# An encoder trunk on one core: operands spread, rows transposed later, factors at the additions, products three key blocks behind scores

## The chip, the core and the metric

The kernel runs on one core of a Trainium2 chip. The core has TensorE (PE), which multiplies matrices into PSUM; VectorE (DVE), ScalarE (ACT) and GpSimd (POOL), which work on rows of 128 partitions; and SyncE (SP), which mostly issues DMAs. Each engine works through its own queue in order, and semaphores let one engine wait for another. The metric is the time of one execution in microseconds (us), as the device tells it.

## What is computed

One layer, 2048 positions of 1024 channels, all in float32. The part of the reference that matters:

```python
xn = rms_norm(x, mix_norm_g[l])
q, k, v, f_logit, z = jnp.split(xn @ w_in[l], [...], axis=-1)
log_f = jax.nn.log_sigmoid(f_logit + b_f[l])
attn = forgetting_attention(q, k, v, log_f)      # 8 heads of 64, causal, logit + c[t] - c[s]
sgu = spatial_gating(jax.nn.gelu(z, approximate=False),
                     sgu_ln_g[l], sgu_ln_b[l], w_s[l], b_s[l])
merged = jnp.concatenate([rms_norm(attn, out_norm_g[l, :D_ATTN]),
                          rms_norm(sgu, out_norm_g[l, D_ATTN:])], axis=-1)
x = x + merged @ w_out[l]
xn = rms_norm(x, ffn_norm_g[l])
gate, up = jnp.split(xn @ w_gate_up[l], 2, axis=-1)
x = x + (jax.nn.silu(gate) * up) @ w_down[l]
return rms_norm(x, final_norm_g)
```

`c` is the running sum of `log_f`. The two `rms_norm`s inside `merged` each give one factor per position: one for the attention half, one for the gating half.

## The kernel before

**Exactness.** A matmul takes operands of a shorter mantissa, so every operand is split into a high part (a cast, L128, on ACT) and a low part (the operand minus the high part, L131, on DVE), and a product is three matmuls: high by high, high by low, low by high.

**Stages.** First q, k, v are projected (to about 310 us of the span). Then follow attention and the gating branch, interleaved (310 to 870 us). The output projection runs from about 870 to 1100 us, overlapping the end of attention. The rest is the feed-forward part, built from seven products per two-by-two block instead of eight (L1742), whose operands are sums and differences of blocks.

**Attention (L727 to L795, loop at L1260).** The loop goes over 320 steps `(head, query chunk of 512, key block of 128)`. In step n, `qk` makes a score tile [128 keys, 512 queries] with two matmuls (L735, L736) into one of two PSUM banks `mx_ps`, which the maxima of later heads (`one_max`, L360) share. ACT takes Exp into `Pt` (L738) and casts it to `Ph` (L128); DVE subtracts to `Pl` (L131); on a diagonal block POOL masks `Ph` and then `Pl` (L748). `pv_of` multiplies by values (L768, L770, L773) into the bank `tp`. It is called `DEPTH` steps after `qk`. `NPH`, `NPL` and `NPT` are the numbers of `Ph`, `Pl` and `Pt` tiles. Keys and values lie in five sets of buffers; `plan_loads` frees a set `DEPTH + 1` steps after its last score, and `keys_until` issues the loads of the next at most `LEAD` = 14 steps ahead of their use. `fin` (L777) closes a head and, after the last head of a chunk, turns the sums into reciprocals (L793) and stores them to `RD` (L794).

**Gating branch.** `gates` (L1008) runs beside attention, paced by n, and fills PE: `z_proj` projects four chunks q, first for the half that is normalised and mixed (`v_side`, stored to `GD`), then for the half that multiplies it (`u_side`, L977). `at_u` (L889) hooks loads to the place `(q, cc, k)` in that projection, among them the load of `GD[q]` into `zvh` (L904), which `u_side` needs at L985. `u_side` multiplies by the mixed half, takes squares, makes the factor `rs`, scales the rows by it (L995), transposes them (L998) and stores them to `ST`.

**Output projection.** `out_prep` loads the transposed rows of one tile of 128 positions (`ST`, `AT`) and the reciprocals, makes the attention half's factor `o["r"]` (squares L1097, sums L1099 and L1100, product L1105) and splits the rows. Tiles 0 and 1 are prepared inside the attention loop from n = `OPEN` = 260 on. `out_tiles` (L1192) runs the products (L1190) in slots of three matmuls, 16 slots a tile; `out_add` (L1179) adds the gating half plainly (L1182) and the attention half times `o["r"]` (L1184). After a tile `out_done` (L1152) stores the row, takes its squares (L1156), its factor (L176), scales it (L1162) and, `NY - 1` calls later, transposes it (L1169) and stores it to `XT` for the feed-forward part. These calls (`posts`) come on every second slot.

**First feed-forward operands.** `first_operands` (L1666) loads the four blocks of the first positions from `XT`, makes the operands R4, R1, R3 in 16 parts spread over the slots, and then R0, R2 and at last R5, R6. The main loop at L1700 calls it on every `FE`-th slot, from tile `FT` = 9 on; what is left is forced when the first half of the last two tiles is done.

**Order.** The framework lays out each engine's queue when the program is built, from the order in which the code issues instructions and from what is ready by its own reckoning. `behind(i, ...)` (L110) keeps what is issued inside it behind i on i's engine.

## Time and profile before

| | us |
|---|---|
| median of 3 runs | 2358.18 (2357.91 to 2358.35) |
| the profiled execution | 2357.63 |
| its span, first to last instruction | 2355.9 |
| PE busy in the span | 2329.2 (99%) |
| DVE busy | 1689.4 (72%) |
| ACT busy | 1059.9 (45%) |
| POOL busy | 607.9 (26%) |
| granted PE clock, mean | 0.998 |

Rows of a group name the line, the engine, the operation, out<-in and its shape, then xcount, busy us, the mean ns of one, and the idle time of the engine just before them with what ended most of it. Rows of the timeline begin with the start and the length in us and end, in brackets, with the idle time before and its releaser. Rows of waits have the total in us, the number of times and the longest. A busy PE is drawn longer than it is, since matmuls are pipelined and their ends modelled. Idle time of an engine that isn't the bound costs nothing by itself.

### The profile page before, as it was taken

What the parts mean: (1) busy time and instruction counts of PE and PEld (TensorE: products, weight loads), DVE (VectorE), ACT (ScalarE), POOL (GpSimd) and SP (SyncE); (2) the same over time, 40 slices, a digit from 0 to 9 for tenths busy, and PEclk for the clock granted to TensorE, in tenths of its full rate; (3) what the DMA queues carried; (4) which work ended last, traced back from release to release, by engine and by line L of the source; (5) the groups of instructions that cost most, each with busy time, mean ns of one, the idle gap of its engine ahead of it and who ended that gap; (6) DMA issues with size and microseconds to landing.
All of it is one profiled execution on the core that took longest, in us unless ns stands there. A gap on an engine that the chain in (4) does not pass through costs nothing.

```text
span 2355.9 us, 31718 instructions
## 1 busy us (share of the span) xinstructions
PE 2329.2 (99%) x10566; PEld 1891.3 (80%) x10566; DVE 1689.4 (72%) x2799; ACT 1059.9 (45%) x1774; POOL 607.9 (26%) x704
## 2 busy tenths in 40 slices
PE   9999999999999999999999999999999999999998
PEld 7778777777777778878888888888888878888886
DVE  6658668888888677567665766866666586685788
ACT  5322138767788776344323233533323252332433
POOL 1100012122211232222322323232323234343431
PEclk9999999999999999999999999999999999999999
DMA  8845667656687775773445544725444355574554
GB/s 271 297 154 189 211 201 208 184 146 169 177 215 239 219 230 178 229 221 126 114 137 162 151 149 129 234 77 145 126 143 143 90 191 193 190 254 170 194 193 150
DMA packets 375947, 423.89 MB, mean 180 GB/s; under 512 B 23956, under 2 KB 277588, under 8 KB 371816
## 3 DMA queue, kind: packets, MB, share of 16 engines
q1 hardware_dynamic: 359800, 378.62, 52.6%
q0 software_dynamic: 7616, 27.33, 3.3%
q10 hardware_dynamic: 8368, 15.91, 1.9%
q8 instruction: 85, 1.39, 0.3%
q14 instruction: 78, 0.64, 0.1%
HBM read 280.87 MB, written 140.91 MB: 179 GB/s over the span
## 4 chain that ended last, share of the span: by engine, by line
PE 89%; DVE 4%; ACT 2%; DMA 2%; issue 2%; POOL 1%; POOLq 0%; ACTq 0%; SPq 0%; DVEq 0%
PE pp L1742 51%; PE mm L575 7%; PE z L927 6%; PE pp L1190 4%; PE mm L457 4%; PE mx_ps L360 2%; PE tp L768 2%; PE tp L773 2%; PE mx_ps L735 2%; PE mx_ps L736 2%; PE oz L1190 2%; PE tp L770 1%; DVE wl L131 1%; DVE Pl L131 1%; PE z L968 0%
## 5 line engine op out<-in xcount | busy, mean ns | idle before, releaser
L128 ACT CAST wh<-raw 128x512 fp32r<-128x512 f32 (+2 forms) x492 | 304.1, 621 | 726.9 <-PE pp L1742 612.9
L131 DVE TENSOR_TENSOR wl<-raw,wh 128x512 fp32r<-128x512 f32 (+2 forms) x496 | 375.7, 765 | 27.5 <-ACT wh L128 27.0
L1742 PE MATMUL pp<-wl,wh 128*128 128x512 f32 x1056 | 325.3, 389 | 1.1 <-ACT u L1490 1.0
L1742 PE MATMUL pp<-wh,wh 128*128 128x512 f32 x1056 | 325.2, 389 | 0.0
L1433 POOL TENSOR_TENSOR raw<-raw 128x512 f32<-128x512 f32 (+1 forms) x124 | 169.2, 1366 | 551.9 <-DMA raw<-in_w_gu_dram 302.5
L131 DVE TENSOR_TENSOR Pl<-Pt,Ph 128x512 fp32r<-128x512 f32 (+1 forms) x320 | 194.9, 614 | 71.6 <-ACT Ph L128 70.4
L1742 PEld LDWEIGHTS pp<-wl,wh 128*128 128x128 f32 x1056 | 198.1, 188 | 42.9 <-ACT u L1490 1.4
L1742 PEld LDWEIGHTS pp<-wh,wh 128*128 128x128 f32 x1056 | 198.2, 188 | 41.0
L738 ACT ACTIVATE Pt<-mx_ps 128x512 f32<-128x512 f32 (+1 forms) x320 | 168.8, 532 | 118.4 <-PE mx_ps L736 112.8
L1742 PE MATMUL pp<-wl,wl 128*128 128x512 f32 x528 | 205.4, 389 | 0.0
L1742 PE MATMUL pp<-wh,wl 128*128 128x512 f32 x528 | 205.4, 389 | 0.0
L1433 DVE TENSOR_TENSOR raw<-raw,raw 128x512 f32<-128x512 f32 (+1 forms) x112 | 136.6, 1221 | 84.1 <-POOL raw L1433 81.0
L927 PE MATMUL z<-wh,xz 128*128 128x512 f32 x496 | 188.7, 397 | 0.0
L128 ACT CAST Ph<-Pt 128x512 fp32r<-128x512 f32 (+1 forms) x320 | 175.5, 556 | 19.7 <-PE tp L770 4.8
L362 DVE TENSOR_REDUCE mx<-mx_ps 128x1 f32<-128x512 f32 x192 | 130.1, 683 | 20.6 <-PE mx_ps L360 19.7
L748 POOL TENSOR_SCALAR_AFFINE_SELECT Ph<-Ph 128x128 fp32r<-128x128 f32 x128 | 51.0, 398 | 300.9 <-DVE Pl L131 252.0
L768 PE MATMUL tp<-Ph,V 128*128 128x512 f32 (+1 forms) x320 | 118.7, 371 | 4.8 <-POOL Ph L748 2.5
L360 PE MATMUL mx_ps<-D,A 66*128 66x512 f32 (+2 forms) x320 | 118.7, 373 | 1.2 <-DVE mx L365 0.8
L773 PE MATMUL tp<-Pl,V 128*128 128x512 f32 (+1 forms) x320 | 118.4, 370 | 1.1 <-POOL Pl L748 1.0
L735 PE MATMUL mx_ps<-A,D 74*128 74x512 f32 (+1 forms) x320 | 118.0, 369 | 1.1 <-ACT Pt L738 1.1
L736 PE MATMUL mx_ps<-B,C 128*128 128x512 f32 (+1 forms) x320 | 117.4, 367 | 0.0
L1742 PEld LDWEIGHTS pp<-wl,wl 128*128 128x128 f32 x528 | 99.1, 188 | 20.6
(355 smaller groups left out, 5287.8 us busy)
## 6 DMA issues: line engine op xcount, KB each, us to landing
raw<-in_w_gu_dram SPq DMA_DIRECT2D x88, 512.0 KB
xz<-XS SPq DMA_DIRECT2D x31, 1024.0 KB
HD<-hT SPq DMA_DIRECT2D x44, 512.0 KB
SM<-xa SPq DMA_DIRECT2D x30, 512.0 KB
D<-KH SPq DMA_DIRECT2D x112, 128.0 KB
XA<-xa SPq DMA_DIRECT2D x27, 512.0 KB
sg<-SM SPq DMA_DIRECT2D x12, 1024.0 KB
raw<-HD SPq DMA_DIRECT2D x24, 512.0 KB
```

Source lines behind the costliest of these rows:

```text
L128: return nc.scalar.copy(o, i) if eng is nc.scalar else eng.tensor_copy(o, i)
L131: return eng.tensor_tensor(o, i, f(h), ALU.subtract)
L360: last_mx.append(nc.tensor.matmul(pm[:, 0:n], lhs, Dt[0 : lhs.shape[0], 0:n], start=True, stop=True))
L575: mm = nc.tensor.matmul(pm, a, b, start=n == 0, stop=n == 3 * KT - 1)
L735: nc.tensor.matmul(st[:, off:], Dt[:, b * P : (b + 1) * P], A[:, off:], start=True, stop=False)
L736: nc.tensor.matmul(st[:, off:], C[:, b * P : (b + 1) * P], B[:, off:], start=False, stop=True)
L738: nc.scalar.activation(Pt[:, off:], st[:, off:], AF.Exp)
L768: nc.tensor.matmul(pv[:, off:], V[:, 0:P], Ph[:, off:], start=kb == 0, stop=False)
L773: nc.tensor.matmul(pv[:, off:], V[:, 0:P], Pl[:, off:], start=False, stop=kb == 4 * j + 3)
L927: nc.tensor.matmul(pz, xz[a][:, k, :], w[b][:, k, :], start=n == 0, stop=n == 3 * KT - 1)
L1433: return (nc.vector if e == "v" else nc.gpsimd).tensor_tensor(o, a, b, op)
L1742: nc.tensor.matmul(pm, a[:, k, :], b[:, k, :], start=on is None and k == 0 and e == 0, stop=k == it.kh - 1 and e == 2, skip_group_check=n ...
```

## The change

It has these parts:

1. `DEPTH` 2 to 3, `NPH` and `NPL` 3 to 4, `NPT` 4 to 3: a product comes three steps behind its score, with four tiles of high and low weights and three of `Pt`. `nd` and `lv` in `fin` share one tile of 128 partitions.
2. `rsg` keeps the gating half's factors of all positions. `u_side` no longer scales rows; `out_add` applies `rsg` to the gating half's product as it applies `o["r"]` to the other's.
3. `NY` 4 to 5, and `posts` also move on at every slot while more than one is waiting: rows are transposed one call later.
4. The first operands start when the first eight tiles' transposed rows are stored, instead of at tile 9, and take a part on every fifth slot. The last sums and R5, R6 are put behind the last row's squares (on ACT) and scaling (on DVE).
5. Tiles 0 and 1 wait six calls instead of four for their loads, and four instead of six between squares and factor. `fin` gives one call between the reciprocal and its store. The loads of `GD[q]` move within the projection.

```diff
-DEPTH = 2
+DEPTH = 3
-NPH = 3
-NPL = 3
+NPH = 4
+NPL = 4
-NPT = 4
+NPT = 3
-NY = 4
+NY = 5
-FT = 9
-FE = 4
+FE = 5
...
+    rsg = T(cst, [P, NB], F32, "rsg")
...
     def fin(h, j):
-        nd, lv = T(p2, [DH, CH], F32, "nd", bufs=1), T(p2, [DH, CH], F32, "lv", bufs=1)
+        both = T(p2, [P, CH], F32, "nd", bufs=1)
+        lv, nd = both[0:DH], both[DH:P]
...
             nc.vector.reciprocal(sr, sr)
+            yield
             ld(RD[j].rearrange("h (a t) -> (h a) t", t=H * CH // P), sr)
...
-        if at[1:] == ((2, 0) if at[0] else (3, 4)):
+        if at[1:] == ((3, 4), (2, 0), (2, 0), (3, 0))[at[0]]:
             m = mixes[at[0]] = T(p2z, [P, 4, CH], F32, "zvh", bufs=1)
             ld(m, GD[at[0]])
...
-        rs = rsqrt(p2, ss, 1.0 / 512, "rs", n=4)
-        yield
+        rsqrt(p2, ss, 1.0 / 512, "rs", n=4, r=rsg[:, 4 * q : 4 * q + 4])
...
         for cc in range(4):
-            nc.vector.tensor_scalar_mul(zr[:, cc, :], zr[:, cc, :], rs[:, cc : cc + 1])
...
-        for _ in range(4):
+        for _ in range(4 if space is None else 6):
             yield
...
             yield from squares()
-            for _ in range(6):
+            for _ in range(4):
                 yield
             yield from factor(p2)
...
-        nc.scalar.activation(xn, xt, AF.Square, accum_out=ss)
+        E["sq"] = nc.scalar.activation(xn, xt, AF.Square, accum_out=ss)
...
-        nc.vector.scalar_tensor_tensor(xn, xt, r, E["ffb"], ALU.mult, ALU.mult)
+        E["xn"] = nc.vector.scalar_tensor_tensor(xn, xt, r, E["ffb"], ALU.mult, ALU.mult)
...
             ld(XT[t // 8][2 * g + q][:, :, sl], xo)
+            E["xt"] = t + g
             yield
...
     def out_add(xs, ps, t, k):
-        if k > 3:
-            nc.vector.tensor_tensor(xs, xs, ps, ALU.add)
-        else:
-            nc.vector.scalar_tensor_tensor(xs, ps, o[t]["r"], xs, ALU.mult, ALU.add)
+        r = rsg[:, t : t + 1] if k > 3 else o[t]["r"]
+        nc.vector.scalar_tensor_tensor(xs, ps, r, xs, ALU.mult, ALU.add)
...
-                        if k % 2 == 0 and posts and next(posts[0], 0) == 0:
+                        if (k % 2 == 0 or len(posts) > 1) and posts and next(posts[0], 0) == 0:
                             posts.pop(0)
...
         yield "wait"
-        tt("v", b11, b11, b12, ALU.add)
-        tt("v", b21, b21, b11, ALU.subtract)
-        R[5] = keep_as(5, b21)
-        R[6] = keep_as(6, b22)
+        with behind(E["sq"], E["xn"]):
+            tt("v", b11, b11, b12, ALU.add)
+            tt("v", b21, b21, b11, ALU.subtract)
+            R[5] = keep_as(5, b21)
+            R[6] = keep_as(6, b22)
         yield "wait"
...
-        if E["t"] >= FT and at is None and m % FE == 0:
+        if E.get("xt", 0) >= NB // 2 and at is None and m % FE == 0:
             at = next(fo)
```

More of the change, by code (lines that the diff above doesn't have):

```diff
@@ L169, in trunk, with rsqrt @@
     nc.vector.memset(mhalf, -0.5)
-    T(cst, [P, 48], F32, "pad")
-    def rsqrt(p, ss, scale, tag, n=1):
+    rsg = T(cst, [P, NB], F32, "rsg")
+    T(cst, [P, 32], F32, "pad")
+    def rsqrt(p, ss, scale, tag, n=1, r=None):
         a = T(p, [P, n], F32, tag + "a")
         nc.vector.tensor_scalar(a, ss, scale, EPS, ALU.mult, ALU.add)
-        r = T(p, [P, n], F32, tag + "r", **({"bufs": 4} if tag == "ra" and p is not p2 else {}))
+        if r is None:
+            r = T(p, [P, n], F32, tag + "r", **({"bufs": 4} if tag == "ra" and p is not p2 else {}))
         nc.gpsimd.tensor_tensor(r, a, mhalf[:, 0:n], ALU.pow)
```

## The prediction, as it was put on record

> **What bounds the kernel now.** I read the busy time of the stages first, then TensorE's (PE's) waits, then the timeline around the longest of them. Columns of the first view: stretch and length in us, then for PE, PE weight load, VectorE (DVE), ScalarE (ACT) and GpSimd (POOL) the busy us with the count of instructions, then granted PE clock, DMA share, GB/s.
>
> ```profile
> 310.00:600.00 290.00, 286.87 (x1356) 226.72 (x1354) 232.50 (x469) 203.24 (x357) 52.79 (x128) 0.99 0.65 178
> 600.00:870.00 270.00, 264.65 (x1262) 205.71 (x1262) 213.85 (x413) 210.06 (x393) 56.99 (x133) 1.00 0.75 215
> 870.00:1100.00 230.00, 226.17 (x1084) 184.92 (x1083) 158.14 (x229) 114.41 (x194) 57.14 (x86) 1.00 0.64 199
> 1100.00:1900.00 800.00, 800.00 (x3531) 662.68 (x3530) 525.71 (x703) 266.88 (x434) 237.11 (x169) 1.00 0.47 137
> ```
>
> PE is the bound everywhere. In the feed-forward stage (from 1100) it never stands: 3531 matmuls in 800 us, one every 0.227 us. Nothing that the change edits runs there, so 800 of the 2355.9 us of the span, and nearly all behind them, can't move. What can be won lies in attention (310 to 870: 3.1 and 5.4 us idle) and in the output projection (870 to 1100: 3.8 us idle).
>
> These idle times are too small as printed. The page's row of the commonest matmul says how much:
>
> ```profile
> L1742 PE MATMUL pp<-wl,wh 128*128 128x512 f32 x1056 | 325.3, 389 | 1.1 <-ACT u L1490 1.0
> ```
>
> A matmul is drawn 0.389 us long but the next starts after 0.227. So each wait costs PE 0.16 us more than its printed idle. The waits of PE, in us in total, times, longest:
>
> ```profile
> PE tp L768 <- POOL Ph L748: 2.5, 7, 0.6
> PE tp L1169 <- DVE xb L1162: 1.9, 1, 1.9
> ...
> PE tp L768 <- ACT Ph L128: 1.3, 1, 1.3
> PE tp L1169 <- DVE xn L1162: 1.2, 2, 0.8
> PE mx_ps L1105 <- POOL zvl L1100: 1.2, 1, 1.2
> PE mx_ps L735 <- ACT Pt L738: 1.1, 3, 0.5
> PE tp L773 <- POOL Pl L748: 1.0, 4, 0.3
> ...
> PE tp L1169 <- DVE raa L174: 0.7, 1, 0.7
> PE tp L768 <- DVE mx L365: 0.7, 1, 0.7
> ```
>
> The reader is to see four families. L768 and L773 multiply weights by values; mostly they wait for POOL's causal mask, the last link behind score, Exp, cast and subtraction. L1169 transposes a finished row and waits for DVE. L1105 and the one wait for ACT belong to the preparation of output rows 0 and 1. L735 is a score that waits for a PSUM bank.
>
> **The change part by part**
>
> *Products three blocks behind.* The length of a score step, from L735's own matmuls:
>
> ```profile
> 400.00:800.00 400.00, 77.92 (x212) 40.00 (x212) 1.00 0.69 193
> ```
>
> 212 scores in 400 us are 1.89 us a step, so DEPTH 3 gives every chain from score to product 1.89 us more. The waits for the mask and the one for DVE's mx are 2.5 + 1.0 + 0.7 = 4.2 us printed, 12 times, so 4.2 + 12 x 0.16 = 6.1 us; the longest is 0.7 + 0.16, well under 1.89. At best 6.1 us go; at worst none, if DVE and ACT stay behind and the wait merely comes later. Stages 310 to 870 keep DVE busy 446 of 560 us, so it can mostly catch up: I take 70%, **4.3 us**. A fourth Ph and Pl tile keeps the cast's relation to the products as it was: both ring and lag grow by one. The five key buffers come free one step later, so their loads are issued 1.89 us later; LEAD lets them go up to 14 steps ahead, and I cost that at nothing.
>
> The waits are followed by a dip of the clock:
>
> ```profile
> 481.00:484.00 3.00, 2.20 (x12) 1.23 (x10) 2.96 (x6) 1.32 (x3) 2.57 (x4) 1.00 0.54 137
> 484.00:488.30 4.30, 4.01 (x13) 2.87 (x12) 3.55 (x7) 3.22 (x6) 0.44 (x1) 0.60 0.38 97
> ```
>
> PE stands 0.8 of 3.0 us waiting for masks, then is granted 0.60 of its clock for 4.3 us: 0.40 x 4.3 = **1.7 us** lost. With the waits gone I count it as won; the other end is nothing. The Trainium skill, "TensorE: Matmul & The Clock Gate", Part 1 on the clock gate, has the clock halve only after a whole idle window of about 3.4 us. By that rule these waits could not be the cause, the dip could stay, and the result would be 1.7 us higher, 2349.7. The rows above show a dip with no idle stretch of that length before it, so the trace speaks against the rule here.
>
> *Rows 0 and 1 prepared two steps later, RD stored one step later.*
>
> ```profile
> SPq L794 <- DVE sr L793: 8.9, 3, 4.4
> ```
> ```profile
> 813.36 3.62 SPq L904 DMA_DIRECT2D zvh<-GD  x1
> ```
> ```profile
> 826.47 0.62 ACT L128 CAST zr<-raw 128x512 fp32r<-128x512 f32 x1 [2.27 <-DMA raw<-ST]
> ...
> 826.99 0.61 ACT L128 CAST Ph<-Pt 128x512 fp32r<-128x512 f32 x1
> ```
> ```profile
> 827.66 0.49 PE L768 MATMUL tp<-Ph,V 128*128 128x512 f32 x1 [1.28 <-ACT Ph L128]
> ```
>
> SyncE's queue stood up to 4.4 us for a reciprocal, with key loads and row 0's own loads queued behind the store; a 1 MB load of GD held it 3.6 us more. ACT then stood 2.27 us at the cast of row 0 for the late data, with the cast of Ph queued behind it, and PE paid 1.28 + 0.16 us; the squares ran late too, so the factor's product (L1105) paid 1.2 + 0.16. Together 2.8 us. Two steps are 3.8 us, more than ACT's 2.27, and the store no longer blocks the queue; but squares to factor shrinks from six to four steps. Between 0 and 2.8 I take **2.0 us**. The GD loads move in the same queue: of q 1, 2 and 3 earlier, of q 0 twelve k steps later. If q 0's comes late, DVE stands in L985 with Pl queued behind. I cost this at nothing, since SyncE reaches that load late already, and bound it by the 3.6 us of the row above, either way.
>
> *Rows transposed later.* NY 5 puts the transposes one post step, two slots of three matmuls, 6 x 0.227 = 1.36 us, further behind. The three waits of L1169 on xn and raa (printed 1.2 + 0.7, at most 0.8 each, 0.96 with the 0.16) fit into that. FE 5 thins the first operands' DVE work, which causes them: 17 parts on every fifth slot end about slot 212, before the 224th, where the rest is forced. Cost of the thinning: nothing; if it slipped past, the rest would run in one burst on DVE.
>
> *The last operands behind the last row.*
>
> ```profile
> 1079.07 2.28 DVE L1433 TENSOR_TENSOR sg<-sg,sg 128x2048 f32<-128x2048 f32 x1
> ...
> 1082.52 2.28 DVE L1433 TENSOR_TENSOR sg<-sg,sg 128x2048 f32<-128x2048 f32 x1
> ...
> 1086.80 2.28 DVE L131 TENSOR_TENSOR wl<-sg,wl 128x2048 fp32r<-128x2048 f32 x1
> ...
> 1089.07 2.28 DVE L131 TENSOR_TENSOR wh<-sg,wh 128x2048 fp32r<-128x2048 f32 x1
> 1091.79 1.28 DVE L1162 SCALAR_TENSOR_TENSOR xb<-xa,r3r,ffb 128x1024 f32<-128x1024 f32 x1 [0.44 <-POOL r3r L176]
> 1092.99 0.69 DVE L131 TENSOR_TENSOR wl<-raw,wh 128x512 fp32r<-128x512 f32 x1
> ```
> ```profile
> 1085.02 0.55 POOL L176 TENSOR_TENSOR r3r<-r3a,mhalf 128x1 f32<-128x1 f32 x1 [15.43 <-DVE r3a L174]
> 1089.30 2.46 POOL L176 TENSOR_TENSOR r3r<-r3a,mhalf 128x1 f32<-128x1 f32 x1 [3.73 <-DVE r3a L174]
> ```
> ```profile
> 1093.22 0.74 PE L1169 MATMUL tp<-ident,xb 128*128 128x128 f32 x5 [1.87 <-DVE xb L1162]
> 1093.73 0.50 PE L1742 MATMUL pp<-R1h,wl 128*128 128x512 f32 x1
> ```
>
> Row 15's factor took POOL 2.46 us beside a large DVE operation and 0.55 without. With the two sums and two low halves (4 x 2.28 = 9.1 us of DVE) held back, xn can start at 1089.30 + 0.55 and end near 1091.1; PE wanted it at 1093.22 - 1.87 - 0.16 = 1091.2. The wait of 1.9 + 0.16 us goes. All four waits of L1169 are 3.8 + 4 x 0.16 = 4.4 us; I take **3.8 us**, since DVE has little slack here.
>
> *Factor at the addition.*
>
> ```profile
> L1184 DVE SCALAR_TENSOR_TENSOR xa<-pp,rar,xa 128x512 f32<-128x512 f32 x14 | 10.5, 748 | 6.7 <-PE pp L1190 5.7 <-POOL rar L176 0.4
> ...
> L1182 DVE TENSOR_TENSOR xa<-xa,pp 128x512 f32<-128x512 f32 x14 | 9.6, 683 | 4.4 <-PE pp L1190 4.4
> L995 DVE TENSOR_SCALAR zr<-zr,rsr 128x512 f32<-128x512 f32 x16 | 7.4, 489 | 1.7 <-POOL rsr L176 1.6
> ```
>
> Sixteen multiplications (7.4 us of DVE) go, and 32 additions grow by 748 - 683 ns (2.1 us). Neither is on PE's path while DVE has room: nothing, though it helps the 70% above.
>
> *Pt ring from four to three.* An Exp now needs the subtraction three steps back to be done. Reading every step, 17 of the 320 start the Exp of step n+3 before the subtraction of step n ends, by 13.9 us in sum. The first and the last of those subtractions, and the worst with its Exp:
>
> ```profile
> 379.36 0.68 DVE L131 TENSOR_TENSOR Pl<-Pt,Ph 128x512 fp32r<-128x512 f32 x1
> ```
> ```profile
> 857.68 0.68 DVE L131 TENSOR_TENSOR Pl<-Pt,Ph 128x512 fp32r<-128x512 f32 x1
> ```
> ```profile
> 626.22 0.55 DVE L131 TENSOR_TENSOR Pl<-Pt,Ph 128x384 fp32r<-128x384 f32 x1
> ```
> ```profile
> 624.53 0.60 ACT L738 ACTIVATE Pt<-mx_ps 128x512 f32<-128x512 f32 x1 [0.64 <-DVE Pl L131]
> ```
>
> The worst would start 2.24 us later. ACT runs in order, so casts and copies queue behind it, and a score then waits for a bank. The cost lies between 0 and 13.9 us. Two mx_ps banks leave an Exp, which ends some 1.3 us after its score starts, up to 2 x 1.89 - 1.3 = 2.5 us, so most late ones are absorbed: I take what such score waits (L735) cost today, 1.1 + 3 x 0.16, **1.6 us**, once more.
>
> **The sum.** 4.3 + 1.7 + 2.0 + 3.8 - 1.6 = 10.2 us. The profiled execution took 2357.63 us (span 2355.9 and 1.7 around it), 0.55 below the median of the runs, 2358.18. From the median: **2348.0 us**. With every wait above gone and nothing given back it is 6.1 + 1.7 + 2.8 + 4.4 = 15.0 us, 2343.2. With six tenths of the 10.2 it is 2352.1. So 2343 to 2352 for the forecast itself.
>
> **The rivals**
>
> *The waits only move.* DVE was busy 446 of 560 us, and in places without a gap; then a later product finds the same backlog and the score waits instead. Only rows 0 and 1 in part (0.5) and L1169 (3.8) are won: 2353.9. Against it: most waits are short and alone. The same time results if the products do not move at all because they are ordered by readiness and not by the loop.
>
> *The held-back block stands before the first operands.* The splits that start at 1092.99 feed the product at 1093.73. If the 9.1 us stay ahead of them, DVE is done at 1091.1 + 9.1 = 1100.2 (up to 1.9 sooner, as ACT is freed as well), while PE, without its wait, asks at 1093.73 - 2.0 = 1091.7: 7 to 9 us. I take 8: 2356.0. For it: the block is written ahead of these splits. Against it: DVE's time from 1079 to 1085 becomes free for them.
>
> *Slower: the ring of three Pt.* Where DVE runs more than two steps behind, Exp, and with it all of ACT, is held to DVE. Should each of the 17 late steps reach PE, 13.9 us are added, and the 4.3 + 1.7 do not come, as the same late subtractions decide them: 2358.2 + 13.9 - 2.0 - 3.8 = 2366.3. It decides from the point where the lateness exceeds the 2.5 us of the banks, less where a maximum's tile takes a bank between two scores. For it: the row at 624.53, where Exp waits for Pl with four tiles already. Against it: the worst case is 2.24.
>
> **How the numbers follow.** Forecast 0.55; waits only move, or products unmoved, 0.20; block before the operands 0.10; ring of three 0.10; more than all the waits above (short stops that are not printed) 0.05. The measurement tells about 0.2%, 4.7 us, from no change: faster means below 2353.5. The forecast and the last case lie there, and half of "waits only move": 0.70. Within: the other half and the block: 0.20. Slower: 0.10. The range leaves out the ring and part of the last case: 2340 to 2360.
>
> **What would show it.** Products: no wait of L768 and L773 for POOL, and no dip of the clock near 485. Rows 0 and 1: ACT not idle for raw<-ST. Transposes: L1169 gone from PE's waits. Block: no wait of L1742 for wl near 1093. Ring: ACT's Exp waiting for Pl, and L735 or L360 for PSUM banks; if that sum grows beyond 5 us, the forecast is wrong. It is wrong as well if the stage from 1100 on gets gaps.

## The result, and the profile after

The changed kernel takes 2353.46 us (median of 22 runs, 2351.36 to 2358.66) against 2358.52 us before (22 runs beside it): a ratio of 0.998, 95% interval 0.9975 to 0.9986. That is 5.1 us faster, inside the range, where the forecast was 10.2 us. It is also within 0.5 us of the first rival's 2353.9 us, but by chance: that rival put nearly all of its gain into the output stage, and the experiments find most of it in attention. The profiled execution has a span of 2352.4 us (2355.9 before).

The stages of the changed kernel, in the columns of the prediction's first view:

```profile
310.00:600.00 290.00, 284.91 (x1346) 224.08 (x1345) 232.98 (x467) 201.78 (x356) 49.81 (x128) 1.00 0.65 178
600.00:870.00 270.00, 269.05 (x1300) 212.92 (x1300) 213.50 (x406) 216.01 (x405) 59.83 (x140) 1.00 0.76 223
870.00:1100.00 230.00, 224.03 (x1069) 182.26 (x1068) 156.44 (x226) 111.30 (x188) 56.19 (x80) 1.00 0.61 188
1100.00:1900.00 800.00, 800.00 (x3531) 662.42 (x3530) 523.65 (x700) 266.10 (x433) 238.33 (x169) 1.00 0.47 139
```

PE's idle time fell from 5.4 to 1.0 us between 600 and 870, but grew from 3.1 to 5.1 between 310 and 600, and from 3.8 to 6.0 in the output projection. The feed-forward stage is untouched. PE's waits, from the same trace (most lines of the file stand one further down than before: L736 is the old L735, L1170 the old L1169):

```profile
PE tp L1170 <- DVE xn L1163: 4.1, 3, 2.2
...
PE pp L1743 <- DVE wl L130: 1.7, 2, 0.9
PE mx_ps L361 <- DVE mx L366: 1.6, 2, 0.8
PE z L971 <- ACT zvh L127: 1.1, 1, 1.1
PE pp L1743 <- ACT u L1535: 1.0, 1, 1.0
...
PE mx_ps L361 <- DVE mx L363: 0.7, 2, 0.4
PE mx_ps L736 <- ACT Pt L739: 0.7, 3, 0.3
...
PE tp L769 <- POOL Ph L749: 0.5, 1, 0.5
PE z L971 <- DVE zr L976: 0.5, 2, 0.3
PE z L971 <- DVE zvl L130: 0.4, 2, 0.2
PE tp L774 <- POOL Pl L749: 0.3, 1, 0.3
```

Of the four families of before, the products (now L769 and L774) and rows 0 and 1 are all but gone, and the scores' wait for a bank (L736) has fallen a little. The transposes are not gone. Two waits are new: L971, the product that mixes strips with the spatial weights (1.1 + 0.5 + 0.4 us), and the one of L1743, the first feed-forward products, for u of L1535 (1.0). Two have grown: L361, the maxima (1.6 + 0.7), and L1743 for wl (1.7). In the kernel before they were these, with 0.3 us more for the maxima:

```profile
PE mx_ps L360 <- DVE mx L365: 0.8, 1, 0.8
PE pp L1742 <- DVE wl L131: 0.8, 1, 0.8
```

### The profile page after: what moved, and what is told of

Same layout as the page of the kernel before. It is cut to its first block, busy times and chain, and to the rows that moved or that the text cites. A ratio compares the mean times of both kernels' runs of the same rounds, so it can differ in the third digit from the quotient of the medians.

```text
span 2352.4 us, 31826 instructions
## 1 busy us (share of the span) xinstructions
PE 2325.9 (99%) x10566; PEld 1889.8 (80%) x10566; DVE 1681.5 (71%) x2783; ACT 1059.0 (45%) x1774; POOL 607.6 (26%) x704
## 4 chain that ended last, share of the span: by engine, by line
PE 72%; DVE 4%; DMA 2%; issue 2%; ACT 1%; POOL 0%; SPq 0%; POOLq 0%; DVEq 0%; ACTq 0%
PE pp L1743 51%; PE z L930 5%; PE pp L1190 2%; PE oz L1190 2%; PE tp L774 2%; PE tp L769 2%; PE mx_ps L737 2%; PE mx_ps L736 2%; PE tp L771 1%; PE mx_ps L361 1%; DVE wl L130 1%; PE z L971 1%; DVE raw L1433 0%; DMA sg<-XT 0%; DVE Pl L130 0%
## 5 line engine op out<-in xcount | busy, mean ns | idle before, releaser
L130 DVE TENSOR_TENSOR wl<-raw,wh 128x512 fp32r<-128x512 f32 (+2 forms) x496 | 370.9, 755 | 26.9 <-ACT wh L127 26.7
L1743 PE MATMUL pp<-wl,wh 128*128 128x512 f32 x1056 | 325.5, 389 | 2.1 <-ACT u L1535 1.0
L1743 PE MATMUL pp<-wh,wh 128*128 128x512 f32 x1056 | 325.2, 389 | 0.0
L1743 PEld LDWEIGHTS pp<-wl,wh 128*128 128x128 f32 x1056 | 198.0, 188 | 44.4 <-ACT u L1535 1.4
L1743 PEld LDWEIGHTS pp<-wh,wh 128*128 128x128 f32 x1056 | 198.1, 188 | 41.2
L1743 PE MATMUL pp<-wh,wl 128*128 128x512 f32 x528 | 205.4, 389 | 0.0
L1743 PE MATMUL pp<-wl,wl 128*128 128x512 f32 x528 | 205.4, 389 | 0.0
L361 PE MATMUL mx_ps<-D,A 66*128 66x512 f32 (+2 forms) x320 | 118.5, 374 | 2.6 <-DVE mx L366 1.6
L736 PE MATMUL mx_ps<-A,D 74*128 74x512 f32 (+1 forms) x320 | 117.9, 369 | 0.8 <-ACT Pt L739 0.7
L774 PE MATMUL tp<-Pl,V 128*128 128x512 f32 (+1 forms) x320 | 117.6, 368 | 0.8 <-POOL Pl L749 0.3
L769 PE MATMUL tp<-Ph,V 128*128 128x512 f32 (+1 forms) x320 | 117.2, 366 | 0.6 <-POOL Ph L749 0.5
L1743 PEld LDWEIGHTS pp<-wl,wl 128*128 128x128 f32 x528 | 99.1, 188 | 20.6
```

The source lines that it names most:

```text
L130: return eng.tensor_tensor(o, i, f(h), ALU.subtract)
L361: last_mx.append(nc.tensor.matmul(pm[:, 0:n], lhs, Dt[0 : lhs.shape[0], 0:n], start=True, stop=True))
L736: nc.tensor.matmul(st[:, off:], Dt[:, b * P : (b + 1) * P], A[:, off:], start=True, stop=False)
L769: nc.tensor.matmul(pv[:, off:], V[:, 0:P], Ph[:, off:], start=kb == 0, stop=False)
L774: nc.tensor.matmul(pv[:, off:], V[:, 0:P], Pl[:, off:], start=False, stop=kb == 4 * j + 3)
L1743: nc.tensor.matmul(pm, a[:, k, :], b[:, k, :], start=on is None and k == 0 and e == 0, stop=k == it.kh - 1 and e == 2, skip_group_check=n ...
```

## The experiments

Each kernel was timed in five rounds beside the kernel before on the same chip. "Ratio" is always to that kernel, with its 95% interval; the changed kernel's is 0.9980 (0.9975 to 0.9986). The medians come from different chips, on which the kernel before took 2357.8 to 2358.9 us, so a difference of 1 us between two of them says nothing; only e2 and e16 have intervals wholly apart from the changed kernel's, and e14's just touches it. One trace can't place effects of 1 or 2 us, so the traces are also compared by stretches: the time between the starts of PE's 1385th and 3800th matmul (some 310 to 820 us), from there to the 4000th (to some 865), and from the 4200th to the 5100th (some 905 to 1100), counted in the trace in order of start. Eight of the kernels (the changed one, e5 to e9, e11, e12) issue PE's first 4000 matmuls in the same order, and e10 shares them with the kernel before. A star marks each dip of the clock in a stretch (last section): one costs about 1.7 us, half of some 3.4 us at half clock.

```
                        1385-3800  3800-4000  4200-5100   median us
before                     513.02*     47.43     193.18     2358.5
e10 output parts           511.41      47.93*    192.42     2357.0
changed kernel             510.07      43.57     195.75     2353.5
e5 sums last               511.25*     47.97**   192.93*    2353.6
e6 NY 4                    509.89      44.73     194.35     2353.3
e7 last free               511.45*     43.30     192.28*    2351.4
e8 every fourth            510.08      46.37*    192.15     2353.2
e9 attention parts         509.87      45.84*    196.57*    2354.6
e11 last one held          510.94*     43.95     190.73     2350.7
e12 last two held          509.68      43.74     192.34*    2351.5
e1 lag of two              513.26*     47.01*    192.66     2355.8
e2 lag of three alone      511.73      49.33*    195.61*    2360.6
e3 rows as before          511.90*     47.31*    192.38     2356.4
e4 rows scaled             511.14      48.17*    192.95     2356.5
e15 step alone             510.36      43.93     192.59     2354.3
e16 multiplications        514.47      45.31     195.10     2359.1
e13 mixing later           508.90*     44.81     197.72*    2350.4
e14 mixing + one held      507.52      45.89*    189.90     2348.6
```

### The parts of attention, one undone or done at a time

e1 undoes the lag, e2 does it alone in the kernel before (with the tile for nd and lv that makes room), e3 undoes the edits of rows 0 and 1, e4 the factor at the additions.

```diff
# e1 against the changed kernel (e2: the reverse, in the kernel before)
-DEPTH = 3
+DEPTH = 2
-NPH = 4
-NPL = 4
+NPH = 3
+NPL = 3
-NPT = 3
+NPT = 4
# e3
-        for _ in range(4 if space is None else 6):
+        for _ in range(4):
...
-            for _ in range(4):
+            for _ in range(6):
...
-            yield
             ld(RD[j].rearrange("h (a t) -> (h a) t", t=H * CH // P), sr)
...
-        if at[1:] == ((3, 4), (2, 0), (2, 0), (3, 0))[at[0]]:
+        if at[1:] == ((2, 0) if at[0] else (3, 4)):
# e4
-        rsqrt(p2, ss, 1.0 / 512, "rs", n=4, r=rsg[:, 4 * q : 4 * q + 4])
+        rs = rsqrt(p2, ss, 1.0 / 512, "rs", n=4)
+        yield
...
+            nc.vector.tensor_scalar_mul(zr[:, cc, :], zr[:, cc, :], rs[:, cc : cc + 1])
...
-        nc.vector.scalar_tensor_tensor(xs, ps, r, xs, ALU.mult, ALU.add)
+        if k > 3:
+            nc.vector.tensor_tensor(xs, xs, ps, ALU.add)
+        else:
+            nc.vector.scalar_tensor_tensor(xs, ps, o[t]["r"], xs, ALU.mult, ALU.add)
```

> The changed kernel with DEPTH 2, three Ph and Pl and four Pt again; all else changed. Theory A (the lag of the products is what the change won between 600 and 850 us): the last score comes 5 to 8 us later than in the changed kernel (937.8 us there), L769's and L774's waits for POOL's mask come back with about 4 us, and the time is 5 to 8 us above the changed kernel's, about that of the kernel before or above it. Rival B (the lag only moved the waits, and the later rows 0 and 1 with the store moved one step won the 7 us): the last score stays within 1.5 us and the time within 2 us of the changed kernel's. A third reading, that the four Pt of DEPTH 2 give something back: 3 us above.

Measured: 2355.77 us, ratio 0.9993 (0.9984 to 1.0002): 2.3 us slower than the changed kernel by the medians, below what theory A asked for, and between rival B's 2 and the third reading's 3. The products' waits are back, as theory A said (L769 for the mask 3.4 us in 6 waits), and L971's wait for zvh is 0.3 us where it was 1.1.

> The kernel before with the lag of three alone (DEPTH 3, four Ph and Pl, three Pt). Theory A: 4 to 7 us faster than before in the time, last score near 939 us (945.5 before), and the clock dip at 485 us is gone. Rival B: within 1.5 us of before, with the products' waits moved to other lines and the dip at most gone (1.7 us).

Measured: 2360.62 us, ratio 1.0008 (0.9999 to 1.0017). Theory A falls: alone, the lag wins nothing and rather loses, 2.8 us by the medians, which is more than rival B allowed too. The waits mostly change places, as these lines of e2's PE waits show:

```profile
PE mx_ps L1106 <- POOL zvl L1101: 2.5, 1, 2.5
...
PE mx_ps L360 <- DVE mx L365: 1.6, 2, 0.8
...
PE tp L768 <- POOL Ph L748: 1.2, 2, 0.6
PE z L969 <- ACT zvh L128: 1.1, 1, 1.1
```

The reader sees the products shrink to 1.2 us, and the factor of row 0 (L1106), the maxima and the mixing product L969 stand in their place.

> The changed kernel with rows 0 and 1 prepared as before (squares to factor six steps, two steps earlier), the store of the reciprocals and the loads of the averages at their old places; the lag of three stays. Theory A: the wait of ACT for row 0's late data near 825 us comes back (2.3 us), PE's waits behind it are shorter than before since the products stand a step further back: 1 to 2.5 us slower than the changed kernel. Rival B: 5 us or more slower, with the last score near 943 us.

Measured: 2356.37 us, ratio 0.9992 (0.9983 to 1.0001), 2.9 us slower than the changed kernel; and ACT stands for row 0's data again, in e3's timeline of ACT:

```profile
825.18 0.62 ACT L127 CAST zr<-raw 128x512 fp32r<-128x512 f32 x1 [1.95 <-DMA raw<-ST]
825.71 0.61 ACT L127 CAST Ph<-Pt 128x512 fp32r<-128x512 f32 x1
```

The size fits theory A's band but for 0.4 us. Its second half doesn't: PE's wait for the factor (L1105) is 2.1 us here, longer than the 1.2 of before. e3 undoes the rows' steps, the store and the loads of GD together, so it doesn't part them.

> The changed kernel with the rows of the long-lag half multiplied by their factor on DVE before the output projection, and plain additions there, as before. Theory A (DVE's time off PE's path costs nothing): within 1.5 us of the changed kernel. Rival C (sixteen multiplications of 0.49 us delay DVE among the scores): 2 to 5 us slower, with more idle of PE waiting for DVE's maxima or low halves between 600 and 850 us.

Measured: 2356.46 us, ratio 0.9993 (0.9984 to 1.0002), 3.0 us slower than the changed kernel. Theory A falls, the size is rival C's: an edit that was costed at nothing is worth as much as the others. The place isn't rival C's: PE waits for the maxima as long as in the changed kernel (1.6 + 0.7 us). e15 and e16 below ask why.

In the table, the stretch from 3800 to 4000, where rows 0 and 1 are made, takes 47.0 to 49.3 us in the kernels that lack any one of the three edits (before, e10, e1 to e4), and 43.3 to 48.0 us in the eight that have all. With 1.7 us taken off for each dip, it is 45.3 to 47.6 against 43.3 to 44.7. So some 2.4 us were won there, by the three together: undoing any one of them loses 1 us or more (e16, which lacks the factor's edit too, stands between with 45.3 and loses more before). In the stretch from 1385 to 3800, with the dips taken off, neither the lag without the factor (e4, 511.1) nor the factor without the lag (e1, 511.6) wins much against before (511.3; e10 511.4), and the eight with both take 509.2 to 510.1. Each of these is one trace.

### The output stage

e5 puts POOL's sums for the first feed-forward products behind the powers of rows 13 to 15. e6 undoes NY 5 with its rule, e7 the bond of the last operands, e8 FE 5.

```diff
# e5
-        r = rsqrt(pev, ss, 1.0 / D, "r3")
+        r, E["r3"] = rsqrt(pev, ss, 1.0 / D, "r3"), rsqrt.last
...
-    make()
+    with behind(E["r3"]): make()
...
# e6
-NY = 5
+NY = 4
-                        if (k % 2 == 0 or len(posts) > 1) and posts and next(posts[0], 0) == 0:
+                        if k % 2 == 0 and posts and next(posts[0], 0) == 0:
# e7
-        with behind(E["sq"], E["xn"]):
+        with behind():
# e8
-FE = 5
+FE = 4
```

The theory came from these lines of the changed kernel, its timelines of POOL and PE:

```profile
1036.04 1.29 POOL L1433 TENSOR_TENSOR raw<-raw 128x512 f32<-128x512 f32 x1 [0.89 <-DMA raw<-in_w_gu_dram]
1037.29 0.55 POOL L177 TENSOR_TENSOR r3r<-r3a,mhalf 128x1 f32<-128x1 f32 x1
```
```profile
1039.31 0.63 PE L1170 MATMUL tp<-ident,xn 128*128 128x128 f32 x4 [2.16 <-DVE xn L1163]
```
```profile
1077.11 1.30 POOL L1433 TENSOR_TENSOR raw<-raw 128x512 f32<-128x512 f32 x1 [13.89 <-DVE r3a L174]
1078.36 0.55 POOL L177 TENSOR_TENSOR r3r<-r3a,mhalf 128x1 f32<-128x1 f32 x1
```
```profile
1080.38 0.63 PE L1170 MATMUL tp<-ident,xn 128*128 128x128 f32 x4 [1.26 <-DVE xn L1163]
...
1093.33 0.50 PE L1743 MATMUL pp<-R3h,wl 128*128 128x512 f32 x1 [0.93 <-DVE wl L130]
...
1099.59 0.73 PE L1743 MATMUL pp<-wl,wh 128*128 128x512 f32 x2 [0.97 <-ACT u L1535]
```

The row's power stands on POOL behind a sum for a later product. PE's wait is put down to DVE's xn, but the link that was late lies one further up the chain.

> The changed kernel with one order changed on POOL: the sums of the first feed-forward operands (1.3 us each) are put behind the powers that give the factors r3r of rows 13 to 15. Theory D (what holds the transposes of L1170 is POOL's queue, where r3r stands behind such a sum): the waits of L1170 near 1036.8 and 1078.7 (2.3 and 1.4 us) shrink to under 1 us together, and the time falls by 2 to 3.5 us against the changed kernel, unless the operands behind the sums then come late (L1743 waiting for wl, over 1.5 us), which takes back as much. Rival E (DVE is late by itself): waits of L1170 unchanged within 0.7 us, time within 1 us.

Measured: 2353.63 us, ratio 0.9981 (0.9971 to 0.9990): no change to the changed kernel. Theory D is right about the wait, and the exception that it named takes the gain back. L1170's waits fall to 0.6 us, from 4.1 in the changed kernel's one trace and 1.3 in those of e1 and e3, which have the same output stage; and a longer wait of L1743 takes over, in e5's PE waits:

```profile
PE pp L1743 <- DVE wl L130: 2.7, 2, 2.1
...
PE tp L1170 <- DVE xn L1163: 0.6, 1, 0.6
```

> The changed kernel with the transposes one post step earlier again (NY 4 and the old rule for posts). The prediction gave the later step 1.36 us per row and 1.9 us in all. Theory D: the waits of L1170 grow from 4.6 us to 7 to 9 us (each of the three waits by up to 1.4), time 2 to 4 us above the changed kernel. Rival F (the later step is what moved the row's end back behind POOL's sum): the waits shrink to under 4 us and the time falls by 1 us or more.

Measured: 2353.26 us, ratio 0.9978 (0.9969 to 0.9987); L1170 waits 3.2 us in all, under rival F's 4, but the time doesn't follow. Neither theory: with the rest in place, the later step makes no difference that shows.

> The changed kernel without the bond that holds the last operands behind the last row. Theory D: POOL's sums then stand again as in the kernel before (no sum between the powers of rows 14 and 15); the wait of 1.42 us at 1078.7 goes or gives place to one of up to 2 us near 1092, as DVE's four large operations run ahead of xn again; the waits of L1743 for wl near 1092 and for u near 1098 go: time within 1 us of the changed kernel. Rival (the held-back block itself is what costs 1.8 us at the change to the feed-forward stage): 1.5 to 2.5 us faster.

Measured: 2351.39 us, ratio 0.9968 (0.9957 to 0.9979), 2.1 us faster than the changed kernel. The rival holds: the bond costs about what the prediction had it win. In e7's trace PE waits 1.9 us for row 15, as before, and none of the three waits near 1080, 1093 and 1099 is there. The stretch from 4200 to 5100 agrees: with the dips taken off, it takes 190.6 us here and in e12, and 190.7 in e11, against 192.4 to 192.9 in the kernels with the changed output stage (e1, e3, e4, e10, e15); the changed kernel's own trace, 195.75, has longer waits of rows besides.

> The changed kernel with the first operands made on every fourth slot again (FE 4, not 5). Prediction: the spreading was costed at nothing for itself and as a help for the rows. Theory D: the sums on POOL stand elsewhere against the powers, and the waits of L1170 change by that alone, by up to 1.3 us a row either way: time within 1.5 us. Rival E (DVE's density of first operands is what makes rows late): waits of L1170 up by 2 us or more and the time by as much.

Measured: 2353.16 us, ratio 0.9974 (0.9964 to 0.9984), no change that shows, as theory D had it.

Then the two halves of the change, each alone in the kernel before (e9 without NY 5, FE 5 and the bond, e10 with these alone).

> The kernel before with the edits of attention alone: lag of three, Pt ring of three, both halves' factors at the additions, rows 0 and 1 later, the store one step later, the averages' loads moved. The output stage's edits (NY 5, FE 5 and its start, the bond of the last operands) are left at their old values. Theory G (attention's edits carry the whole gain, the output stage's give some of it back): 6 to 8 us faster than before (2350 to 2352), the wait of 2.0 us of L1170 for row 15 is there as before, and L1743's waits of 1.1 us near 1092 and 1098 are not. Rival H (the edits of the output stage pay as the prediction has it, 3.8 us): 1 to 2 us faster than before at most.

Measured: 2354.60 us, ratio 0.9987 (0.9978 to 0.9996): 3.7 us faster than the kernel before beside it, less than theory G asked for and more than H. With NY 4 and FE 4 together the rows' waits are back, in e9's timeline of PE:

```profile
1027.33 0.63 PE L1170 MATMUL tp<-ident,xn 128*128 128x128 f32 x4 [1.53 <-DVE xn L1163]
...
1052.45 0.63 PE L1170 MATMUL tp<-ident,xn 128*128 128x128 f32 x4 [0.74 <-DVE xn L1163]
```

e7 differs from e9 by NY 5 and FE 5 with its start alone and is 3.2 us faster by the medians. So the two together are worth that, and one of them seems to be enough: undone singly, with the bond in place (e6, e8), nothing is lost that shows.

> The kernel before with the output stage's edits alone (NY 5 and its rule, FE 5 and its start, the bond of the last operands behind row 15). Theory G: 0 to 3 us slower than before: row 15's wait of 2.03 us goes, and a wait of 1.4 us for row 14 behind POOL's sum, one of 1.1 for wl and one of 1.1 for u come, 1.6 us net. Prediction and rival H: 3.8 us faster than before.

Measured: 2357.01 us, ratio 0.9994 (0.9985 to 1.0003): neither slower, nor 3.8 us faster, and its interval reaches no change. The waits at the border to the feed-forward stage are those theory G named, printed 1.3, 0.7 and 1.0 us.

What is left of the bond's idea is to hold back less of it. e11 holds one large low half behind row 15, e12 both low halves.

```diff
# e11
-        with behind(E["sq"], E["xn"]):
-            tt("v", b11, b11, b12, ALU.add)
-            tt("v", b21, b21, b11, ALU.subtract)
-            R[5] = keep_as(5, b21)
+        tt("v", b11, b11, b12, ALU.add)
+        tt("v", b21, b21, b11, ALU.subtract)
+        R[5] = keep_as(5, b21)
+        with behind(E["xn"]):
             R[6] = keep_as(6, b22)
# e12: the line of R[5] inside as well
```

> The changed kernel with only the last of the four large DVE operations of the first operands held behind row 15; the two sums and one low half run freely. From the trace with none held: row 15's normalisation then starts about 1.3 to 2.2 us sooner (its power takes 0.55 us and not 2.46 beside a large operation), so PE's wait of 2.0 us for row 15 falls to 0 to 0.8 and none of L1743's waits near 1092 and 1098 come. Theory G: 1 to 2.5 us faster than with none held, 3.5 to 5.5 us faster than the changed kernel (2348 to 2350). Rival I (what is held at all comes too late for the first feed-forward products): the same as the changed kernel.

Measured: 2350.74 us, ratio 0.9969 (0.9958 to 0.9980): 2.7 us faster than the changed kernel, no more than with none held (e7). So theory G's 3.5 to 5.5 us didn't come, nor did rival I's standstill. Row 15's wait is gone and so is that for u; one of 0.92 us for wl stays. e11's timeline of DVE shows the order that does it:

```profile
1081.23 2.28 DVE L130 TENSOR_TENSOR wh<-sg,wh 128x2048 fp32r<-128x2048 f32 x1
1083.43 0.14 DVE L174 TENSOR_SCALAR r3a<-ss 128x1 f32<-128x1 f32 x1
1083.50 0.68 DVE L130 TENSOR_TENSOR wl<-raw,wh 128x512 fp32r<-128x512 f32 x1
1084.62 1.29 DVE L1163 SCALAR_TENSOR_TENSOR xb<-xa,r3r,ffb 128x1024 f32<-128x1024 f32 x1 [0.44 <-POOL r3r L177]
1085.82 2.29 DVE L130 TENSOR_TENSOR wl<-sg,wl 128x2048 fp32r<-128x2048 f32 x1
```

> The changed kernel with both large low halves held behind row 15 and only the two sums free. Theory G: DVE reaches row 15 with no large operation ahead, so its wait is under 0.5 us unless POOL's first sum (1.3 us or more) stands ahead of its power again, then 0.7 to 1.4; the two low halves (4.6 us) run after the first splits and before the products that need them, so no wait for wl over 1 us: 3 to 6 us faster than the changed kernel. Rival I: L1743 waits 1 us or more for wl near 1092 and for u near 1098 as in the changed kernel; no gain.

Measured: 2351.54 us, ratio 0.9976 (0.9967 to 0.9985), 1.9 us faster than the changed kernel by the medians, with the intervals overlapping. Row 15 waits no more, but L1743 waits 2.48 us for wl: rival I's wait, grown.

### Where the lag's gain went

e13 and e14 give the mixing products one step of the side work more, e14 together with e11's edit.

```diff
# e13
+        yield
         wst_h, wst_l = ZC["wst"]
```

> The changed kernel with the mixing products (L971) one step of the side work later. Theory J (the lag's waits moved there): L971's waits, 2.0 us printed in the changed kernel with 1.1 the longest near 494, fall under 0.6 us, and the stretch from matmul 1385 to matmul 3800 (510.0 us where no clock dip falls into it) takes 508 to 509 us; time 1 to 2 us below the changed kernel. Rival K (DVE's backlog is the bound there): the wait of 1.1 us turns up within 20 us at another line (L361, L736 or a product), and the stretch stays at 510.

Measured: 2350.40 us, ratio 0.9969 (0.9959 to 0.9980), 3.1 us faster than the changed kernel. Theory J holds, with a larger gain than its 1 to 2 us: L972 (L971 before this edit) waits 0.5 us in all, no wait of 1.1 us follows within 20 us, and the stretch from 1385 to 3800 takes 508.90 us though a clock dip falls into it (507.2 without).

> The mixing products one step later and only the last large low half held behind row 15. Theory J: 1 to 2 us below the kernel with the last one held alone (2350.7), so 2348.5 to 2350. Rival K: the same as that kernel, 2350 to 2351.5.

Measured: 2348.58 us, ratio 0.9961 (0.9947 to 0.9975): 9.8 us below the kernel before and the fastest of all; its stretch from 1385 to 3800 is 507.52 us, 2.5 less than the changed kernel's. The wait in question, from the changed kernel's timelines of PE and DVE:

```profile
495.77 0.39 PE L971 MATMUL z<-zvh,wsth 128*128 128x256 f32 x1 [1.09 <-ACT zvh L127]
```
```profile
493.00 0.84 DVE L959 SCALAR_TENSOR_TENSOR zr<-zr,mv,lngb 128x512 f32<-128x512 f32 x1
493.77 0.64 DVE L130 TENSOR_TENSOR Pl<-Pt,Ph 128x384 fp32r<-128x384 f32 x1
494.33 0.74 DVE L960 SCALAR_TENSOR_TENSOR zr<-zr,rlr,lnbb 128x512 f32<-128x512 f32 x1
```

PE no longer stops at the products and so comes to the mixing earlier, while DVE, without a gap here, still has the strip's last quarter to normalise between its subtractions of Pl. The mixing step wasn't tried with a lag of two, but L971's wait comes with the lag: 1.1 us for zvh in e2 and the changed kernel, 0.3 in e1.

### What the factor at the addition is worth, and why

e4 put back two things, sixteen multiplications and a step between the factor's power and them. e15 puts back the step alone, e16 the multiplications alone.

```diff
# e15
         rsqrt(p2, ss, 1.0 / 512, "rs", n=4, r=rsg[:, 4 * q : 4 * q + 4])
+        yield
# e16: e4 without its yield
```

> The changed kernel with one step more between the squares of a strip and its transposes, and no multiplication. Theory L (what the edit won is the step: rows 0 and 1 are made one step sooner and their data is there when ACT asks): 2 to 3 us slower than the changed kernel, the first transposes of the strip begin near 685 as in the kernel before (678.0 in the changed one), and the stretch from matmul 3800 to 4000 takes 47 to 48.5 us (43.3 to 46.4 with the edit in). Rival M (DVE's time is what counts): within 1 us of the changed kernel.

Measured: 2354.32 us, ratio 0.9982 (0.9973 to 0.9991): the changed kernel's time within 1 us. Theory L, mine, falls.

> The changed kernel with the sixteen multiplications and plain additions as before, but without the step between the factor's power and them. Theory L: within 1 us of the changed kernel, with the strip's first transposes near 678 and the stretch from matmul 3800 to 4000 at 43.3 to 46.4 us. Rival M: 2 to 3 us slower, since DVE stands at the first multiplication for POOL's power (0.5 us, four times) and each of the sixteen takes 0.49 us among the scores; then the stretch from matmul 1385 to 3800 is 511 us instead of 510.

Measured: 2359.09 us, ratio 1.0001 (0.9992 to 1.0010), 5.6 us slower than the changed kernel; the stretch from 1385 to 3800 grows by 4.4 us. Rival M is right that DVE's time counts, at about twice the size that it gave, and the multiplications do need the step. e16's PE waits, and ACT's timeline at the longest:

```profile
PE z L1000 <- ACT wsth L1003: 2.0, 1, 2.0
...
PE z L1000 <- DVE zr L997: 1.4, 2, 1.2
```
```profile
757.80 0.59 ACT L1003 COPY wsth<-z 128x512 f32<-128x512 f32 x1 [3.72 <-DMA ST<-wsth]
```

L1000 transposes the strip that DVE has just multiplied. In the wait of 1.2 us DVE's multiplication stands for POOL's power, as rival M had it. The wait of 2.0 is another: ACT can't copy a transposed strip into `wsth` before the store of the last one from there has landed. So without the step the multiplications stand in a chain that PE waits for. That doesn't explain e4, where the step is in place and PE waits only 0.5 us for a multiplied strip: of its 3.0 us some 1 lies in the stretch to 3800 and, with the dip taken off, some 2.4 where rows 0 and 1 are made. How the multiplications reach that place isn't shown, only that it isn't by the step (e15).

## Why the prediction was wrong in size

**Products three behind** (4.3 us, and 1.7 for the clock). This step failed, in its size: 6.0 us were forecast, and about 1.5 us came in the stretch in question. That the chains get their step is right: printed waits of L768 and L773 for POOL, 2.8 + 1.0 us in e10's trace, are 0.5 + 0.3 in the changed kernel. That DVE "can mostly catch up" is wrong. In runs with no clock dip, the stretch from 310 to 820 us fell from 511.4 (e10) to 509.9 us (the mean of the changed kernel, e6, e8, e9 and e12, 509.7 to 510.1): 1.5 us. The kernel before fits, 513.0 with its dip of 1.7. The rest went to L971 and L361, as the first rival said, but only in part. e2 (1.0008) shows that the lag alone wins nothing, e4 that without the factor's edit it wins little in this stretch (511.1), and e14 that 2.5 us of the loss lay at L971. L361's part wasn't tried.

**The clock dip** was counted as the waits' effect. It isn't bound to them, as the two stretches of e10, with the order and the waits of the kernel before, show:

```profile
481.00:484.00 3.00, 2.20 (x10) 1.32 (x9) 2.96 (x6) 1.21 (x2) 2.00 (x3) 1.00 0.37 96
484.00:488.30 4.30, 4.03 (x19) 2.99 (x19) 3.82 (x7) 3.73 (x7) 1.01 (x2) 1.00 0.45 126
```

PE is busy 2.20 of 3.0 us, as before, and the clock stays at 1.00. In the kernels that share the changed kernel's order of matmuls, dips fall elsewhere or not at all: near 552 us in e5, e7 and e11, between 830 and 840 in e5, e8 and e9, and nowhere before 870 in the changed kernel, e6 and e12. So 1.7 us were booked for an event of chance.

**Rows 0 and 1** (2.0 us): right in mechanism and about in size; e3 gives 2.9 us, with the store and the loads of GD in it. ACT no longer stands for raw<-ST. What the step missed is that DVE's sum on the same row now waits for RD's copy, which lands at other times from run to run: ACT then idles between 0.28 (the changed kernel) and 2.56 us (e5) for the same order of work.

**The Pt ring** (1.6 us lost): ACT's Exp does come late more often, standing 7.0 us for DVE's Pl in nine places (1.2 in three before), but PE's wait for Pt is 0.7 us in the changed kernel and 1.6 in e5, 0.5 and 1.1 in e10 and before. Its cost is small; no run separates it. The slower rival did not come.

**Factor at the addition** (nothing): wrong. It is worth 3.0 us (e4), which hides that the lag is worth less. The step took DVE's time to be free wherever DVE has room. It wasn't: e16 shows the waits that follow without the step, while e4's, with it, are found only in part.

**Rows transposed later** (the three waits on xn and raa, 1.8 of the 3.8 us with the 0.16s taken in part): right in mechanism and larger, 3.2 us from e9 to e7, with FE 5 in it, and either edit seems to be enough. The trace of the changed kernel happens to show such waits again (its POOL sum at 1036.04 ahead of the power), where e1, e3, e5 and e8 have few.

**The last operands behind the last row** (2.0 us): this step failed in its sign. Row 15's wait of 2.03 us goes, as forecast. In its place come 1.42 us for row 14, whose power now has POOL's sum ahead of it, 1.09 for wl, and 1.13 for u: 3.64 us (printed waits and 0.16 each). The changed kernel's DVE and ACT:

```profile
1092.59 2.50 DVE L130 TENSOR_TENSOR wl<-raw,wh 128x512 fp32r<-128x512 f32 x4
```
```profile
1098.43 0.62 ACT L127 CAST wh<-raw 128x512 fp32r<-128x512 f32 x1 [2.10 <-PE pp L1743]
```

Three of the four large operations, from 1085.98 us on, stand ahead of the first splits, which is wl's wait. u's copy stands behind a cast that itself stood 2.10 us for PE; why u comes late is open. The second rival named the wl and put it at 8 us; it was 1.09 with two companions. e7, without the bond, is 2.1 us faster.

Together: 6.4 us were forecast for attention and 3.7 measured with these parts alone (e9), 3.8 for the output stage and 1.3 measured (e10, not clear of nothing); their sum, 5.0, is the 5.1 of the whole. On the rule of the Trainium skill ("TensorE: Matmul & The Clock Gate", Part 1 on the clock gate): by it these short waits can't cause a dip, and the dip at 485 could stay. No dip is at 485 in the changed kernel's trace, but e10 has none there with all the waits either, so that case decides nothing. Against the rule stand the dips that follow a single short stop (last section).

## What to carry to other kernels

A wait that is removed is worth something only as far as the engine behind it has time: where DVE has no gap, PE meets the same backlog at its next product, so look for the next place at which PE asks for that engine and give it slack in the same edit (lag and mixing step together were worth about what the lag alone was to bring: 511.6 us in e1, with its dip taken off, and 507.5 in e14, in the stretch from 310 to 820). A block of work that is held back for one consumer must be followed on every engine that it uses (here DVE, ACT and POOL) to its own consumer; holding the last quarter of it ended the wait that holding all was meant to end, without two of the three new ones, though the time is no better than with none held. And work on an engine with room isn't free for that: sixteen multiplications, 7.4 us of DVE's time and costed at nothing, were worth 3 us.

## What the hardware showed that was not expected

TensorE's granted clock halves for some 3.4 us at a time (e5's near 832 lasts twice that), and with the same order of matmuls it does so in one run and not in another. Two stretches of e5, in the columns of the windows above, and the same two of the changed kernel:

```profile
828.00:832.00 4.00, 2.49 (x9) 1.10 (x8) 4.00 (x6) 3.32 (x7) 2.53 (x3) 0.95 0.65 149
832.00:838.00 6.00, 6.00 (x17) 4.83 (x18) 4.75 (x8) 3.72 (x8) 2.56 (x6) 0.50 0.31 126
```
```profile
828.00:832.00 4.00, 4.00 (x21) 3.24 (x22) 4.00 (x7) 3.65 (x8) 1.33 (x2) 1.00 0.39 164
832.00:838.00 6.00, 6.00 (x33) 4.82 (x33) 3.13 (x9) 3.86 (x8) 4.18 (x10) 1.00 0.24 72
```

17 matmuls in 6 us against 33. But for one at the very end of each kernel, the dips follow stops, none of them over 2.7 us, and begin between 0.4 us before PE resumes and 2.1 us after. In e7's timeline of PE, where the start of a matmul every 0.23 us is the full rate:

```profile
1087.39 0.74 PE L1170 MATMUL tp<-ident,xb 128*128 128x128 f32 x5 [1.88 <-DVE xb L1163]
...
1088.23 0.40 PE L1743 MATMUL pp<-R1h,wh 128*128 128x512 f32 x1
1088.46 0.59 PE L1743 MATMUL pp<-R1l,wh 128*128 128x512 f32 x1
1088.85 0.63 PE L1743 MATMUL pp<-R1h,wl 128*128 128x512 f32 x1
1089.28 0.63 PE L1743 MATMUL pp<-R1h,wh 128*128 128x512 f32 x1
```

One stop of 2.04 us, and from 1088.46 on the matmuls start 0.43 us apart, some eight times. In the kernel before, the like stop of 2.03 us before 1093.22 was followed by no dip. So a stop that is removed spares at times 1.7 us more than itself, and a single trace can mislead by some us: e5's profiled execution took 2357.43 us where its median is 2353.63.
